# One core's transformer network: the last weight sum of a chunk's last pair on VectorE, and the activations' block sums queued behind the norm's factor

## The chip, the core and the metric

The kernel runs on one core of a Trainium2 chip. The core has a matrix engine (PE, TensorE), a vector engine (DVE, VectorE), an activation engine (ACT, ScalarE), a general engine (POOL, GpSimd) and a sync engine (SP) that here only issues DMAs. Each engine works through its own queue in order; between engines an instruction waits on semaphores. The metric is the device time of one execution in microseconds (us); less is better.

## The reference, cut to what matters

Input is a sequence of 512 tokens of width 1024. A first block (sparse attention beside an mLSTM, cross attention, one SwiGLU network) is followed by a second block of two layers, each with a half-step SwiGLU network ahead of its mixer and one behind it. The change is in three of these four networks: numbers 1, 2 and 4 in the order in which they run (`BLOCKED`). Each computes

```
h = h + 0.5 * swiglu(rms_norm(h, gain))
def swiglu(x, w_gate, w_up, w_down):      # x 512 x 1024, F = 2816
    return (silu(x @ w_gate) * (x @ w_up)) @ w_down
```

The rms norm is split: the gain goes into the activations, and the factor per token is multiplied in behind the products. Everything is float32.

## The kernel before, in words

**Exact products.** A float32 operand is split into a high and a low part (`split`, L125 to L136): ACT makes the high part (`whi` of a weight, `xh` or `sh` of activations; L129, L135), DVE the low part (`wlo`, `xl`, `sl`; L133, L136). A product is three matmuls (`mm3`, L175). So every weight tile of 128x1024 costs one ACT and one DVE instruction before PE can use it.

**The blocked networks** (`ffn_blocks`, L385 to L584). The hidden width is 22 row tiles. The first four (p = 0 to 3) are projected plainly, each as a gate product `pg` and an up product `pu` over the 512 tokens (24 matmuls of 512 columns each), and finished by `plain` (L507): DVE multiplies the gate by the factor `rb` (L510), ACT applies Silu (L511), DVE multiplies by the up part (L512), and the result is split into `hh` and `hl`. The other tiles are computed in pairs (`pair`, L465) by a 2x2 block scheme with seven products in place of eight: tokens are halved (LO, HI), and the width too. Seven products of 24 matmuls with 256 columns go to PE for a pair m, with sums of weights on one side and sums of activation blocks (`s1` to `s4`) on the other: s1 with the weight sum `wt`; a11 with b11; s4 with b22; then, behind the last product of the pair before, s2 with `wt` after a second sum; a12 with b21 (PSUM tile B, `sc`); s3 with b12; and last a22 with `wt` after a third sum.

**The weight sum.** `wt` is one SBUF tile that changes twice. `sum_ahead` (L501) makes the first value on DVE. `add` (L436) then adds a block in place by DMAs with accumulation, issued by POOL, two of 256 KB each: `add(wt, m, 3)` behind the split for s1, `add(wt, m, 2)` behind the split for s2 (L485). The block that the last one adds, b21, is also loaded by SP into a tile of its own for the product B (`load`, L429). After each change the tile is split again. A chunk is a run of pairs between two down projections: pairs 2 to 3, 4 to 7, 8 to 10; so there are nine chunk ends in the three networks, with m = 3, 7, 10. At a chunk's end no pair follows whose products would lie between s3 and a22.

**The block sums.** `block_sums` (L405) makes the raw sums r1 to r4 of the activation blocks on DVE (L410 to L414), in two halves `kp`, and splits them into `sh` and `sl`. It needs only the new activations, so the scheduler puts it wherever DVE is free, which is before the norm's factor is there.

**What sets the order.** PE's order is written out by hand around the pairs (`order_pe`, `free_pe`). DVE, ACT, POOL and SP get theirs from a list scheduler with a cost model; `tc.issue_after(instruction)` keeps what is issued inside it behind that instruction. The norm's factor comes from a chain (`inv_rms_chain`, L232): sums of squares by matmuls with `ones` (L259), a power on POOL (L265), transposes with `ident` (L272), and the copy `rb` to SBUF on DVE (L245).

Of the kernel before, what the change touches and what calls it, by code (L numbers as in the profile page):

```python
# [12 lines left out]
ALU = mybir.AluOpType  # L13
# [3 lines left out]
D = 1024  # L17
# [33 lines left out]
def kernel(ctx: ExitStack, tc: tile.TileContext, t: dict, out: bass.AP):  # L51
    nc = tc.nc
# [44 lines left out]
    xa, x = load_x()  # L97
# [19 lines left out]
    def v(name, j):  # L117
        o = VOFF[name] + j
        return vec[:, o : o + 1]
# [115 lines left out]
    def inv_rms_chain(state, first, second):  # L235

        if not state:
            for j in range(KT):
                square_acc(x[j], j, state, eng=nc.vector)
        got = []  # L240

        def finish():
            rt, pb = rms_rows(got[0], WHOLE)
            rb = act_p.tile([P, S], F32, tag="rb", bufs=2, name=nm("rb"))
            nc.vector.tensor_copy(rb, pb)  # L245
            got[:] = [rt, rb]

        chain.append([first, lambda: got.append(rms_sums(state, 1e-6, WHOLE))])
        chain.append([second, finish])
        return got  # L250
# [131 lines left out]
    LO, HI = HALVES  # L382
    CHUNKS = ((0, 4), (4, 8), (8, FT // 2))

    def ffn_blocks(fp, xs, st, gname, wg, wu, wd, out_cb, head=2, tail=0, step=None):  # L385
# [12 lines left out]
        sums = {}  # L398
# [5 lines left out]

        def block_sums(kp):  # L405
            r1, r2, r3, r4 = (raw[q, kp] for q in (1, 2, 3, 4))
            for kk in range(2):
                k, c = 2 * kp + kk, slice(256 * kk, 256 * kk + 256)
                g1, g2 = v(gname, k), v(gname, 4 + k)
                nc.vector.tensor_scalar(r1[:, c], x[4 + k][:, HI], g2, None, ALU.mult)  # L410
                nc.vector.scalar_tensor_tensor(r1[:, c], x[k][:, HI], g1, r1[:, c], ALU.mult, ALU.subtract)
                nc.vector.scalar_tensor_tensor(r2[:, c], x[k][:, LO], g1, r1[:, c], ALU.mult, ALU.subtract)
                nc.vector.scalar_tensor_tensor(r4[:, c], x[4 + k][:, LO], g2, r2[:, c], ALU.mult, ALU.subtract)
                nc.vector.tensor_tensor(r3[:, c], x[k][:, LO], x[k][:, HI], ALU.subtract)  # L414
            split(r1, *sums[1, kp])
            split(r2, *sums[2, kp], -1.0)
            split(r4, *sums[4, kp])
            for kk in range(2):
                c = slice(256 * kk, 256 * kk + 256)
                split(r3[:, c], *(t_[:, c] for t_ in sums[3, kp]), v(gname, 2 * kp + kk))  # L420

# [42 lines left out]

        def pair(m, p):  # L465

# [17 lines left out]
            product(A, s2, load_w(None, D, wt), False)  # L484
            add(wt, m, 2)  # L485
            nc.vector.tensor_tensor(of_half(c2, 0), of_half(c2, 0), lanes(A), ALU.subtract)
            B = ps_tile("sc")
            product(B, a12, load_w(None, D, load(m, 2)), True)
            nc.vector.tensor_tensor(of_half(c1, 0), of_half(c1, 0), lanes(B), ALU.add)
# [52 lines left out]
        for p in range(4):  # L542
            if p < len(pss):
                pg, pu = pss[p]
            else:
                pg = mm_tile()
                proj(pg, load_w(wg[p], D), xs)
                pu = at_tile()
                proj(pu, load_w(wu[p], D), xs)
            plain(p, pg, pu)  # L550
            if p in (2, 3):
                block_sums(p - 2)
        for ci, (m0, m1) in enumerate(CHUNKS):
            last = ci == len(CHUNKS) - 1
            ms = range(max(m0, 2), m1)
            for p in range(len(hs) if ci == 0 else 0, 2 * (m1 - m0)):
                if ci == 0:
                    hs.append(h_tiles(p))
                else:
                    hs[p:p + 1] = [h_tiles(p)]  # L560
            gens = {m: pair(m, 2 * (m - m0)) for m in ms}
            order_pe()
# [109 lines left out]
    free_pe()  # L672
    rt, rb = got
    for ps, nme in zip(first, ("kc", "vc")):
# [883 lines left out]
    free_pe()  # L1558
    rt, rb = got
    Wl, PTs = None, []  # L1560
# [179 lines left out]
```

## Time and profile before

| what | us |
|---|---|
| median of 3 runs | 2802.57 |
| lowest and highest run | 2800.8, 2808.41 |
| the profiled execution's own time | 2799.68 |
| its span in the trace | 2797.9 |
| PE busy | 2707.0 |
| DVE busy | 1732.4 |
| ACT busy | 1214.6 |
| POOL busy | 439.5 |

The span is what the trace covers of the profiled execution; some 2 us lie around it. The mean granted clock of TensorE is 0.986 of full speed. Busy times overlap across engines, and only what PE waits for shows directly in the time.

### The profile page before, as it was taken

The numbers are of one execution on the slowest core, as the hardware profiler recorded it, in microseconds if no ns is written. First come the engines' busy times: TensorE is split into PE (matmuls) and PEld (weight loads), VectorE is DVE, ScalarE is ACT, GpSimd is POOL, SyncE is SP. The second block draws the span as 40 slices with busy tenths as digits, with TensorE's granted clock in tenths as the row PEclk, the third lists the DMA queues.
The fourth block names the chain that finished last, engine by engine and source line by source line (L and its number), as shares of the span: only waits on it lengthen the run. The fifth ranks groups of instructions, "written<-read, shape, count | busy, mean of one in ns | idle before, by whom it ended". The sixth has DMA issues, their size and how long they took to land.

```text
span 2797.9 us, 40467 instructions
## 1 busy us (share of the span) xinstructions
PE 2707.0 (97%) x15856; PEld 2332.1 (83%) x15856; DVE 1732.4 (62%) x2608; ACT 1214.6 (43%) x1967; POOL 439.5 (16%) x559
## 2 busy tenths in 40 slices
PE   9999999999998999999899999999999998999998
PEld 6877988888887898986688989898888874899997
DVE  7666564642437666669885666744444489666665
ACT  6676544422334434442344434443222366443434
POOL 0133132100002110122220101200000136211112
PEclk9999999999998999999999999999999999999999
DMA  6313321323322454536333545323232320254552
GB/s 201 98 47 99 120 68 53 98 80 111 97 84 97 121 129 117 135 112 163 96 117 106 144 121 123 111 89 100 83 113 89 100 69 8 81 132 116 140 131 73
DMA packets 118051, 291.84 MB, mean 104 GB/s; under 512 B 13111, under 2 KB 20279, under 8 KB 117860
## 3 DMA queue, kind: packets, MB, share of 16 engines
q1 hardware_dynamic: 100700, 258.43, 29.1%
q0 software_dynamic: 15552, 28.32, 6.6%
q10 hardware_dynamic: 1608, 2.52, 0.3%
q8 instruction: 124, 2.03, 0.3%
q14 instruction: 67, 0.55, 0.1%
HBM read 284.91 MB, written 4.30 MB: 103 GB/s over the span
## 4 chain that ended last, share of the span: by engine, by line
PE 67%; DVE 9%; DMA 4%; issue 4%; ACT 2%; POOL 0%; SPq 0%; DVEq 0%; ACTq 0%; POOLq 0%
PE mm L175 23%; PE sc L175 19%; PE tr L175 17%; PE po L175 6%; DMA wb<-wu 3%; DVE wlo L133 2%; ACT whi L129 1%; DVE c L1340 1%; DVE rm L1507 1%; DVE xl L136 1%; DVE conv L1340 1%; PE po L1537 1%; DMA R<-glscr 0%; DMA glscr<-gl 0%; PE sc L160 0%
## 5 line engine op out<-in xcount | busy, mean ns | idle before, releaser
L129 ACT ACTIVATE whi<-wraw 128x1024 fp32r<-128x1024 f32 (+3 forms) x386 | 370.4, 970 | 756.4 <-PE sc L175 248.5
L133 DVE TENSOR_TENSOR wlo<-wraw,whi 128x1024 fp32r<-128x1024 f32 (+4 forms) x451 | 450.9, 1015 | 283.3 <-ACT whi L129 282.7
L175 PE MATMUL mm<-xh,whi 128*128 128x256 f32 (+1 forms) x1016 | 334.7, 330 | 5.9 <-ACT whi L129 5.9
L129 ACT ACTIVATE whi<-wb 128x1024 fp32r<-128x1024 f32 x189 | 199.9, 1058 | 321.7 <-PE mm L175 86.5
L175 PE MATMUL mm<-xl,whi 128*128 128x256 f32 (+1 forms) x1016 | 333.8, 329 | 5.5 <-DVE xl L136 5.5
L175 PE MATMUL mm<-xh,wlo 128*128 128x256 f32 (+1 forms) x1016 | 333.7, 328 | 0.0
L133 DVE TENSOR_TENSOR wlo<-wb,whi 128x1024 fp32r<-128x1024 f32 x189 | 230.8, 1221 | 111.3 <-ACT whi L129 107.2
L175 PEld LDWEIGHTS mm<-xh,whi 128*128 128x128 f32 x1016 | 194.7, 192 | 23.3 <-ACT whi L129 6.5
L175 PEld LDWEIGHTS mm<-xl,whi 128*128 128x128 f32 x1016 | 194.8, 192 | 22.3 <-DVE xl L136 6.8
L175 PEld LDWEIGHTS mm<-xh,wlo 128*128 128x128 f32 x1016 | 194.8, 192 | 15.9 <-DVE wlo L133 0.5
L175 PE MATMUL sc<-xh,whi 128*128 128x512 f32 (+1 forms) x576 | 200.8, 349 | 0.0
L175 PE MATMUL sc<-xh,wlo 128*128 128x512 f32 (+1 forms) x576 | 199.8, 347 | 0.0
L175 PE MATMUL sc<-xl,whi 128*128 128x512 f32 (+1 forms) x576 | 199.8, 347 | 0.0
L438 POOL DMA_DIRECT2D wb<-wg x54 | 47.2, 874 | 745.2 <-DVE wlo L133 739.5
L218 POOL TENSOR_TENSOR sqacc<-sq,sq 128x512 f32<-128x512 f32 (+1 forms) x11 | 16.7, 1516 | 862.0 <-issue 671.6
L175 PE MATMUL mm<-sh,whi 128*128 128x256 f32 (+1 forms) x448 | 132.6, 296 | 19.9 <-ACT c L453 18.9
L175 PE MATMUL tr<-xl,whi 128*128 128x512 f32 (+1 forms) x416 | 147.7, 356 | 3.9 <-DVE xl L136 3.9
L175 PE MATMUL tr<-xh,whi 128*128 128x512 f32 (+1 forms) x416 | 148.5, 357 | 1.0 <-ACT xh L135 1.0
L175 PE MATMUL tr<-xh,wlo 128*128 128x512 f32 (+1 forms) x416 | 147.8, 355 | 0.0
L175 PE MATMUL mm<-sl,whi 128*128 128x256 f32 (+1 forms) x448 | 132.7, 296 | 0.0
L175 PE MATMUL sc<-hh,whi 128*128 128x512 f32 (+1 forms) x347 | 132.5, 382 | 0.0
L175 PE MATMUL mm<-sh,wlo 128*128 128x256 f32 (+1 forms) x448 | 132.1, 295 | 0.0
(573 smaller groups left out, 7114.2 us busy)
## 6 DMA issues: line engine op xcount, KB each, us to landing
wraw<-wg SPq DMA_DIRECT2D x56, 512.0 KB, 3.5
wraw<-wu SPq DMA_DIRECT2D x56, 512.0 KB, 3.5
wb<-wg SPq DMA_DIRECT2D x108, 256.0 KB, 4.2
wb<-wu SPq DMA_DIRECT2D x108, 256.0 KB, 5.0
wraw<-wd SPq DMA_DIRECT2D x56, 384.0 KB, 3.0
wraw<-wd SPq DMA_DIRECT2D x56, 320.0 KB, 2.9
wb<-wg POOLq DMA_DIRECT2D x54, 256.0 KB, 4.1
wb<-wu POOLq DMA_DIRECT2D x54, 256.0 KB, 7.4
```

What stands on the lines that cost most here:

```text
L129: last_hi[0] = nc.scalar.activation(hi[:, sl], src[:, sl], AF.Copy)
L133: nc.vector.tensor_tensor(lo[:, sl], src[:, sl], f32(hi[:, sl]), ALU.subtract)
L136: nc.vector.scalar_tensor_tensor(lo, src, scale, f32(hi), ALU.mult, ALU.subtract)
L175: nc.tensor.matmul(ps, a, b, start=start and c == 0, stop=stop and c == 2, skip_group_check=more)
L218: eng.tensor_tensor(state["acc"][:, ts], state["first"][:, ts], sq[:, ts], ALU.add)
L438: nc.gpsimd.dma_start(w[:, 512 * lane : 512 * lane + 512], src, accum_op=ALU.add)
L1340: nc.vector.scalar_tensor_tensor(d, tap(k), v("w_dw", 31 * j + k), d, ALU.mult, ALU.add)
L1507: nc.vector.tensor_tensor_scan(rm[:, :L][:, ::-1], ob[:, 1 : L + 1][:, ::-1], ob[:, 1 : L + 1][:, ::-1], 1.0, ALU.mult, ALU.bypass)
L1537: nc.tensor.matmul(po[64 * hx : 64 * hx + 64, j * P :], vsh[:, j, c0 : c0 + 64], PTs[hx][:, o : o + n_], start=j == 0, stop=j == NT - 1)
```

## The change

The copy `rb` is handed out of the norm's chain as an instruction. `block_sums` takes a list of steps (half, part), and it is called with all DVE and ACT instructions kept behind that copy: r1 of both halves at p = 2; at p = 3 r2 and r4 of both halves (r4 is split first), then r3. In `pair`, a flag marks a chunk's last pair; there the third value of `wt` is made by a DVE addition of the loaded b21, and the two accumulating DMAs are not issued.

```diff
@@ -242,8 +242,7 @@
         def finish():
             rt, pb = rms_rows(got[0], WHOLE)
             rb = act_p.tile([P, S], F32, tag="rb", bufs=2, name=nm("rb"))
-            nc.vector.tensor_copy(rb, pb)
-            got[:] = [rt, rb]
+            got[:] = [rt, rb, nc.vector.tensor_copy(rb, pb).ins]
 
         chain.append([first, lambda: got.append(rms_sums(state, 1e-6, WHOLE))])
         chain.append([second, finish])
@@ -402,22 +401,26 @@
         def h_tiles(p):
             return [fp.tile([P, S], F32R, tag=f"h{q}{p}", name=nm(f"h{q}{p}")) for q in "hl"]
 
-        def block_sums(kp):
-            r1, r2, r3, r4 = (raw[q, kp] for q in (1, 2, 3, 4))
-            for kk in range(2):
-                k, c = 2 * kp + kk, slice(256 * kk, 256 * kk + 256)
-                g1, g2 = v(gname, k), v(gname, 4 + k)
-                nc.vector.tensor_scalar(r1[:, c], x[4 + k][:, HI], g2, None, ALU.mult)
-                nc.vector.scalar_tensor_tensor(r1[:, c], x[k][:, HI], g1, r1[:, c], ALU.mult, ALU.subtract)
-                nc.vector.scalar_tensor_tensor(r2[:, c], x[k][:, LO], g1, r1[:, c], ALU.mult, ALU.subtract)
-                nc.vector.scalar_tensor_tensor(r4[:, c], x[4 + k][:, LO], g2, r2[:, c], ALU.mult, ALU.subtract)
-                nc.vector.tensor_tensor(r3[:, c], x[k][:, LO], x[k][:, HI], ALU.subtract)
-            split(r1, *sums[1, kp])
-            split(r2, *sums[2, kp], -1.0)
-            split(r4, *sums[4, kp])
-            for kk in range(2):
-                c = slice(256 * kk, 256 * kk + 256)
-                split(r3[:, c], *(t_[:, c] for t_ in sums[3, kp]), v(gname, 2 * kp + kk))
+        def block_sums(steps):
+            for kp, part in steps:
+                r1, r2, r3, r4 = (raw[q, kp] for q in (1, 2, 3, 4))
+                for kk in range(2):
+                    k, c = 2 * kp + kk, slice(256 * kk, 256 * kk + 256)
+                    g1, g2 = v(gname, k), v(gname, 4 + k)
+                    if part == 1:
+                        nc.vector.tensor_scalar(r1[:, c], x[4 + k][:, HI], g2, None, ALU.mult)
+                        nc.vector.scalar_tensor_tensor(r1[:, c], x[k][:, HI], g1, r1[:, c], ALU.mult, ALU.subtract)
+                    elif part == 2:
+                        nc.vector.scalar_tensor_tensor(r2[:, c], x[k][:, LO], g1, r1[:, c], ALU.mult, ALU.subtract)
+                        nc.vector.scalar_tensor_tensor(r4[:, c], x[4 + k][:, LO], g2, r2[:, c], ALU.mult, ALU.subtract)
+                    else:
+                        nc.vector.tensor_tensor(r3[:, c], x[k][:, LO], x[k][:, HI], ALU.subtract)
+                        split(r3[:, c], *(t_[:, c] for t_ in sums[3, kp]), g1)
+                if part == 1:
+                    split(r1, *sums[1, kp])
+                elif part == 2:
+                    split(r4, *sums[4, kp])
+                    split(r2, *sums[2, kp], -1.0)
 
         def of_sum(q):
             return [tuple(t_[:, 256 * (k % 2) : 256 * (k % 2) + 256] for t_ in sums[q, k // 2]) for k in range(4)]
@@ -462,7 +465,8 @@
 
         first_sum = {}
 
-        def pair(m, p):
+        def pair(m, p, ends):
+
 
             if m not in first_sum:
                 first_sum[m] = sum_ahead(m)
@@ -482,10 +486,14 @@
             nc.scalar.activation(of_half(c2, 0), lanes(E), AF.Copy)
             yield
             product(A, s2, load_w(None, D, wt), False)
-            add(wt, m, 2)
+            if not ends:
+                add(wt, m, 2)
             nc.vector.tensor_tensor(of_half(c2, 0), of_half(c2, 0), lanes(A), ALU.subtract)
             B = ps_tile("sc")
-            product(B, a12, load_w(None, D, load(m, 2)), True)
+            b21 = load(m, 2)
+            product(B, a12, load_w(None, D, b21), True)
+            if ends:
+                nc.vector.tensor_tensor(wt, wt, b21, ALU.add)
             nc.vector.tensor_tensor(of_half(c1, 0), of_half(c1, 0), lanes(B), ALU.add)
             if m + 1 < FT // 2:
                 first_sum[m + 1] = sum_ahead(m + 1)
@@ -548,8 +556,9 @@
                 pu = at_tile()
                 proj(pu, load_w(wu[p], D), xs)
             plain(p, pg, pu)
-            if p in (2, 3):
-                block_sums(p - 2)
+            if p >= 2:
+                with tc.issue_after(got[2]):
+                    block_sums([(0, 1), (1, 1)] if p == 2 else [(0, 2), (1, 2), (0, 3), (1, 3)])
         for ci, (m0, m1) in enumerate(CHUNKS):
             last = ci == len(CHUNKS) - 1
             ms = range(max(m0, 2), m1)
```

Two further lines take `got[:2]` where `got` was unpacked.

At a chunk's end on DVE, first network, pair 3, before: `wlo_1659` is the low part of `wt` (`wb_1640`) for s2, `wlo_1663` that of b21, `wlo_1668` that of b12 for s3, `wlo_1670` that of the final `wt`; L486 takes s2's product out of PSUM.

```order
L133 TENSOR_TENSOR wlo_1659_9039<-wb_1640_8865,whi_1658_9038 128x1024
L454 TENSOR_TENSOR c_1624_8705<-c_1624_8705 128x512
L133 TENSOR_TENSOR wlo_1663_9074<-wb_1661_9070,whi_1662_9073 128x1024
L133 TENSOR_TENSOR hl5_1615_8689<-c_1624_8705,hh5_1614_8688 128x512
L133 TENSOR_TENSOR wlo_1668_9111<-wb_1642_8869,whi_1667_9110 128x1024
L133 TENSOR_TENSOR wlo_1670_9145<-wb_1640_8865,whi_1669_9144 128x1024
L452 TENSOR_TENSOR c_1623_8704<-c_1623_8704,rb_1567_8507 128x512
L486 TENSOR_TENSOR c_1646_8908<-c_1646_8908,mm_1650_8941 128x2x256
```

The same place with the change:

```order
L133 TENSOR_TENSOR wlo_1659_9039<-wb_1640_8865,whi_1658_9038 128x1024
L457 TENSOR_TENSOR c_1624_8705<-c_1624_8705 128x512
L496 TENSOR_TENSOR wb_1640_8865<-wb_1640_8865,wb_1661_9068 128x1024
L133 TENSOR_TENSOR wlo_1663_9072<-wb_1661_9068,whi_1662_9071 128x1024
L133 TENSOR_TENSOR hl5_1615_8689<-c_1624_8705,hh5_1614_8688 128x512
L133 TENSOR_TENSOR wlo_1668_9110<-wb_1642_8869,whi_1667_9109 128x1024
L133 TENSOR_TENSOR wlo_1670_9144<-wb_1640_8865,whi_1669_9143 128x1024
L455 TENSOR_TENSOR c_1623_8704<-c_1623_8704,rb_1567_8507 128x512
L491 TENSOR_TENSOR c_1646_8908<-c_1646_8908,mm_1650_8941 128x2x256
```

The addition (L496) stands three instructions ahead of where the final `wt` is split, and L486 is now L491; the rest keeps its order.

At the head of network 4 on DVE, from the copy `rb` on, before (L510 and L512 are `plain`'s multiplications of p = 0, 1, 2):

```order
L245 COPY rb_3699_22189<-po_3698_22184 128x512
L510 TENSOR_TENSOR c_3724_22234<-mm_3683_21933,rb_3699_22189 128x512
L510 TENSOR_TENSOR c_3727_22242<-mm_3685_21935,rb_3699_22189 128x512
L512 TENSOR_TENSOR c_3724_22234<-tr_3684_21934,c_3724_22234 128x512
L512 TENSOR_TENSOR c_3727_22242<-tr_3686_21936,c_3727_22242 128x512
L133 TENSOR_TENSOR hl0_3726_22239<-c_3724_22234,hh0_3725_22238 128x512
L133 TENSOR_TENSOR hl1_3729_22247<-c_3727_22242,hh1_3728_22246 128x512
L510 TENSOR_TENSOR c_3730_22250<-sc_3687_22131,rb_3699_22189 128x512
L133 TENSOR_TENSOR wlo_3762_22422<-wb_3753_22379,whi_3761_22421 128x1024
L512 TENSOR_TENSOR c_3730_22250<-sc_3688_22132,c_3730_22250 128x512
```

With the change the copy is followed by r1's first halves and r3 (eight instructions L411 and L417) and the two L518 that were L510 of p = 0 and 1; then:

```order
L412 SCALAR_TENSOR_TENSOR sraw_3700_22204<-x_789_3625,vec_73,sraw_3700_22204 128x256 x2
L412 SCALAR_TENSOR_TENSOR sraw_3712_22216<-x_789_3625,vec_73,sraw_3712_22216 128x256 x2
L136 SCALAR_TENSOR_TENSOR sl30_3708_22212<-sraw_3706_22210,vec_73,sh30_3707_22211 128x256 x2
L136 SCALAR_TENSOR_TENSOR sl31_3720_22224<-sraw_3718_22222,vec_73,sh31_3719_22223 128x256 x2
L414 SCALAR_TENSOR_TENSOR sraw_3703_22207<-x_789_3625,vec_73,sraw_3700_22204 128x256
L133 TENSOR_TENSOR wlo_3762_22416<-wb_3753_22373,whi_3761_22415 128x1024
L414 SCALAR_TENSOR_TENSOR sraw_3703_22207<-x_789_3625,vec_73,sraw_3700_22204 128x256
L520 TENSOR_TENSOR c_3724_22228<-tr_3684_21928,c_3724_22228 128x512
L414 SCALAR_TENSOR_TENSOR sraw_3715_22219<-x_789_3625,vec_73,sraw_3712_22216 128x256
L520 TENSOR_TENSOR c_3727_22236<-tr_3686_21930,c_3727_22236 128x512
L414 SCALAR_TENSOR_TENSOR sraw_3715_22219<-x_789_3625,vec_73,sraw_3712_22216 128x256
L133 TENSOR_TENSOR sl10_3702_22206<-sraw_3700_22204,sh10_3701_22205 128x512
```

All 30 DVE instructions of a network's block sums stand behind `rb` now, with `plain`'s multiplications and the weights' low parts between them; the first low part for s1 (`sl10`) is the twenty-sixth instruction behind the copy, and the last multiplication of p = 3 (L520) stands behind all of them.

On ACT, at the place where pair 2 of network 4 hands on its first PSUM tiles: `hh3` is the high part of p = 3, L478 copies the product a11 with b11 (`mm_3760`) out of the PSUM tile that s2 then continues, and L475 and L482 copy E (`tr_3757`). Before:

```order
L511 ACTIVATE c_3741_22340<-c_3741_22340 128x512
L129 ACTIVATE whi_3766_22483<-wb_3752_22378 128x1024
L129 ACTIVATE hh3_3742_22344<-c_3741_22340 128x512
L129 ACTIVATE whi_3770_22518<-wb_3769_22515 128x1024
L475 ACTIVATE c_3756_22387<-tr_3757_22388 128x2x256
L129 ACTIVATE whi_3775_22555<-wb_3754_22382 128x1024
L478 ACTIVATE c_3755_22386<-mm_3760_22420 128x2x256
L129 ACTIVATE whi_3780_22592<-wb_3772_22547 128x1024
```

With the change (L482 is what L478 was, L486 what L482 was):

```order
L519 ACTIVATE c_3730_22244<-c_3730_22244 128x512
L519 ACTIVATE c_3741_22326<-c_3741_22326 128x512
L129 ACTIVATE hh2_3731_22248<-c_3730_22244 128x512
L129 ACTIVATE whi_3780_22586<-wb_3772_22541 128x1024
L486 ACTIVATE c_3756_22381<-tr_3757_22382 128x2x256
L129 ACTIVATE hh3_3742_22330<-c_3741_22326 128x512
L482 ACTIVATE c_3755_22380<-mm_3760_22414 128x2x256
```

`hh3` stood four places ahead of the copy that frees s2's PSUM tile, and now stands right ahead of it; both Silu (L519) and `hh2` have come into this stretch. On PE, networks 1 and 2 now run s1, a11 and the first seven matmuls of s4 ahead of p = 3's up product, which stood behind the first three matmuls of s1; the rest of PE's order stays.

## Rows read from the trace of the kernel before

**Rows 1.** The page, part 1: busy us of each engine, share, instructions.

```profile
PE 2707.0 (97%) x15856; PEld 2332.1 (83%) x15856; DVE 1732.4 (62%) x2608; ACT 1214.6 (43%) x1967; POOL 439.5 (16%) x559
```

**Rows 2.** Waits of PE, whole span: line and releaser: us, times, longest.

```profile
PE mm L175 <- ACT c L453: 18.9, 6, 4.7
PE sc L259 <- DVE sqacc L220: 7.5, 1, 7.5
```

**Rows 3.** Timeline of PE at two chunk ends: start, duration, instruction [idle before].

```profile
962.56 0.36 PE L175 MATMUL mm<-sh,whi 128*128 128x256 f32 x1 [2.33 <-ACT c L453]
...
1642.28 0.55 PE L175 MATMUL mm<-sh,whi 128*128 128x256 f32 x1 [4.68 <-ACT c L453]
...
1647.33 0.42 PE L175 MATMUL mm<-sh,wlo 128*128 128x256 f32 x1
```

**Rows 4.** Windows of PE: stretch, length, busy (count), granted clock, DMA share, GB/s.

```profile
900.00:915.00 15.00, 12.24 (x50) 0.75 0.29 74
...
1085.00:1100.00 15.00, 11.59 (x64) 0.89 0.51 166
1506.00:1520.00 14.00, 11.31 (x67) 0.88 0.35 110
1640.00:1660.00 20.00, 17.72 (x89) 0.83 0.28 86
...
2635.00:2655.00 20.00, 17.30 (x92) 0.91 0.32 98
```

**Rows 5.** Timeline of DVE at the first chunk end.

```profile
948.58 1.22 DVE L133 TENSOR_TENSOR wlo<-wb,whi 128x1024 fp32r<-128x1024 f32 x1
...
959.99 1.23 DVE L133 TENSOR_TENSOR wlo<-wb,whi 128x1024 fp32r<-128x1024 f32 x1 [6.10 <-ACT whi L129]
...
961.73 0.68 DVE L486 TENSOR_TENSOR c<-c,mm 128x512 f32<-128x512 f32 x1
```

**Rows 6.** Timeline of ACT there: b21's high part, then the final sum's.

```profile
949.24 1.04 ACT L129 ACTIVATE whi<-wb 128x1024 fp32r<-128x1024 f32 x1
...
958.89 1.06 ACT L129 ACTIVATE whi<-wb 128x1024 fp32r<-128x1024 f32 x1 [5.78 <-DMA wb<-wu]
```

**Rows 7.** Timeline of POOL there: the two accumulating DMAs' issues.

```profile
950.10 0.87 POOL L438 DMA_DIRECT2D wb<-wg  x1 [11.43 <-DVE wlo L133]
950.64 1.22 POOL L438 DMA_DIRECT2D wb<-wu  x1
```

**Rows 8.** Timeline of PE at the heads of networks 1, 2 and 4.

```profile
902.76 1.84 PE L259 MATMUL sc<-ones,sqacc 128*128 128x1 f32 x8 [7.50 <-DVE sqacc L220]
...
920.05 0.28 PE L175 MATMUL tr<-sh,whi 128*128 128x256 f32 x1
...
934.14 0.28 PE L175 MATMUL mm<-sh,whi 128*128 128x256 f32 x1
...
1482.96 0.28 PE L175 MATMUL mm<-sh,whi 128*128 128x256 f32 x1
...
2478.48 0.28 PE L175 MATMUL tr<-sh,whi 128*128 128x256 f32 x1
...
2481.36 0.28 PE L175 MATMUL mm<-sh,whi 128*128 128x256 f32 x1
```

**Rows 9.** Timeline of DVE: block sums of network 1, and two copies `rb`.

```profile
894.33 0.68 DVE L133 TENSOR_TENSOR sl<-sraw,sh 128x512 fp32r<-128x512 f32 x1
894.93 0.47 DVE L413 SCALAR_TENSOR_TENSOR sraw<-x,vec,sraw 128x256 f32<-128x256 f32 x1
895.33 0.68 DVE L136 SCALAR_TENSOR_TENSOR sl<-sraw,sh 128x512 fp32r<-128x512 f32 x1
...
910.94 0.68 DVE L245 COPY rb<-sc 128x512 f32<-128x512 f32 x1
...
2460.20 0.69 DVE L245 COPY rb<-po 128x512 f32<-128x512 f32 x1 [1.92 <-PE po L272]
```

**Rows 10.** Groups by line, DVE, 881 to 903.5 us: count | busy us, mean ns.

```profile
L410 DVE TENSOR_SCALAR sraw<-x,vec 128x256 f32<-128x256 f32 x4 | 1.4, 340 | 0.0
```

More of the change, by code (lines that the diff above doesn't have):

```diff
@@ L560, in ffn_blocks @@
                     hs[p:p + 1] = [h_tiles(p)]
-            gens = {m: pair(m, 2 * (m - m0)) for m in ms}
+            gens = {m: pair(m, 2 * (m - m0), m == ms[-1]) for m in ms}
             order_pe()
@@ L672 @@
     free_pe()
-    rt, rb = got
+    rt, rb = got[:2]
     for ps, nme in zip(first, ("kc", "vc")):
@@ L1558 @@
     free_pe()
-    rt, rb = got
+    rt, rb = got[:2]
     Wl, PTs = None, []
```

## The prediction

> **What bounds the kernel now.** I read the page first. PE is busy for 2707.0 us of the span [rows 1], so an edit on another engine can gain only what PE waits for, and can lose whatever new wait it makes. Next I read the list of PE's waits [rows 2]. Two entries touch lines of this change: a product's matmuls waiting six times, 18.9 us in all, by a release put down to an ACT copy (L453), and one wait of 7.5 us for the sums of squares.
>
> The timeline of PE shows where the six are: two of them, 2.33 and 4.68 us, are the first matmul of s3 in a chunk's last pair [rows 3]. All six are of that form, in the first and second chunk of each network; the third chunk's end has none. The name L453 misleads, since that copy is done before anyone can need it. The queues around the first end tell the true cause. DVE splits `wt` for s2 at 948.58 [rows 5], POOL issues the two accumulating DMAs at 950.10 and 950.64 [rows 7], and ACT sits idle for 5.78 us with the final sum's high part at the head of its queue, until 958.89, released by the DMA [rows 6]. DVE, behind it, starts the low part at 959.99 after 6.10 us of idleness, and only then, at 961.73, takes s2's product out of PSUM (L486) [rows 5]. s3 overwrites that PSUM tile, so PE starts at 962.56. The final sum itself is needed later: it holds up the wrong instruction by standing ahead of it in two queues.
>
> A wait also costs clock. The windows show full speed lost around the ends: granted clock 0.89, 0.88, 0.83 and 0.91 [rows 4]. After 4.68 us of waiting the 24 matmuls of s3 take from 1642.28 to 1647.33 plus a last one of some 0.2 [rows 3], 5.26 us, where an undisturbed product of that form takes 2.88 (from 2478.48 to 2481.36) [rows 8]. One minus the clock, times the length of the window, is 1.65 + 1.68 + 3.40 + 1.80 = 8.5 us for the four windows; part of it lies in the waits themselves. Counted by the matmuls behind the waits I take 7.
>
> **Part A, the addition on DVE.** Eighteen accumulating DMAs and their issues go, nine additions of 128x1024 come. I price one by the low part of a weight, the same form with two inputs: 1.22 us [rows 5], of which the next instruction overlaps 0.08, so 1.14. b21 is no new wait: ACT makes its high part at 949.24 already [rows 6], so it has landed when the addition runs at about 950.4. Queued behind the addition stand the low parts of b21 and b12, the final `wt`, and L486. The final sum is ready at 951.6. Counting back from 960, where B ends and PE comes to s3, by 2.88 a product, s2 ran from 954.3 to 957.2. The final sum's high part then waits only for a buffer that frees when a22 of the pair before ends, at 954.3; with 1.04 for it, 1.22 for the low part and 0.6 for the multiplication ahead of L486, DVE comes to L486 at 957.3, as s2's product is just there, and PSUM is free at about 958. So the wait goes whole at this end, with about 2 us to spare, and the 1.14 us of DVE are covered by that slack; without it they would cost 1.14 at each of six ends. Since the others have the same queues, all six go. b21's load buffer comes free about 1.2 us later, which delays a weight load of the down projection; I cost that at nothing for the same slack, and at most at 1.2 us each. So part A brings 18.9 us if the clock gives nothing back, 27 with the windows' 8.5, 26 with 7; I take 26, since a clock that fell behind a wait has no such cause left.
>
> The two DMAs of one sum end some 8.2 us after the second issue (950.64 to 958.89) [rows 6, 7]; that is the duration used. The Trainium skill, DMA: Bandwidth & Descriptors, section on the anatomy of one DMA by the gpsimd path, gives 2.0 us plus bytes over 436e3, for 256 KB an estimate of 2.6 us. By that the sum would be there at 953.3, before its buffer, part A would be worth nothing, and the total would be the heads' loss alone. The trace does not agree, and the measurement decides.
>
> **Part B, the block sums behind `rb`.** What it removes: in network 1 these sums ran ahead of the squares on DVE, and PE waited 7.50 us at 902.76 for the squares [rows 8], in a window at a clock of 0.75 [rows 4], so 3.75 us of full speed, most of it in the wait; about 1.5 lies behind it. Up to 9 us go there, less what the last squares wait for on their own account.
>
> What it adds: 30 DVE instructions between the copy `rb` and the pairs. Prices as start to start: 0.60 for 512 columns (894.33 to 894.93), 0.40 for 256 (894.93 to 895.33) [rows 9], 0.26 for the one-input form (340 ns less 0.08) [rows 10], 1.14 for a weight. In order of the queue up to s1's second low part: copy 0.6, four L411 1.04, four L417 1.6, two L518 1.2, four L412 1.6, four low parts of r3 1.6, four L414 1.6, a weight 1.14, two L520 1.2, two low parts of r1 1.2: 12.8 us, and 12.2 to the first.
>
> In **network 1** the copy starts at 910.94 [rows 9], so s1 can start at 923.1; PE wanted it at 920.05 [rows 8], and now has no up product in between: 3.1 us of wait. Up to the first low part of r4 follow four L415 1.6, two weights 2.28 and five of 512 columns 3.0: 19.7 us, at 930.6. PE, done with s1 and a11 (2.88 each) from 923.1 on, is there at 928.9: 1.7 more. Behind the up product and the rest of s4, s2 waits about 0.3 for the copy out of its PSUM tile, which stands behind `hh3` on ACT. s2 comes about 5.1 us late against 934.14 [rows 8], up to 6.2 with some clock lost. Against the 7.5 to 9 removed I take minus 3, between minus 4 and 0, since I can't see when the last squares are ready.
>
> **Network 2** has the same queue, s2 at 1482.96 before [rows 8], and no wait to lose: 5.1 to 6.4 us, I take 6.
>
> In **network 4** the copy starts at 2460.20 [rows 9]. The whole queue to the last multiplication of p = 3 adds, to the 12.8, six weights 6.84, ten of 512 columns 6.0 and four L415 1.6: 27.2 us, at 2487.4. Here the up product is done early, so nothing fills the gaps: s4, wanted at 2478.48 [rows 8], waits about 2.5 for its first low part, 1.5 for its second. Then on ACT `hh2`, a weight's high part (1.04 [rows 6]), two PSUM copies and `hh3` at 0.5 to 0.6 each lie between that multiplication and s2: 2489.9 against 2481.36 [rows 8], 8.5 late, a last wait of 4.5. At the chunk ends waits of such a length took clock; with that, 7 to 11 us, I take 9.5.
>
> Sum: 26 gained, 3 gained, 6 and 9.5 lost, so 13.5 off 2799.68, the profiled execution's own time: 2786.2. The median of the runs lies 2.9 above that execution: **2789**. By the bounds (27 + 4 - 5 - 7 = 19, and 19 + 0 - 6.4 - 11 = 1.6) between 2783.5 and 2801 as medians.
>
> **The rivals.**
>
> *The heads eat the gain.* The ends return only their waits, network 1 gains nothing, and 2 and 4 cost their upper bounds: 1.6 off, 2801, within 0.3% (8.4 us, about what a measurement of this kernel can tell from no change). For it: every number of part B is a queue sum in which one late ACT step adds. Against: the waits at the ends are whole and the slack is 2 us. It decides once the ends give under 19 or the heads cost over 20.
>
> *The heads cost nothing.* DVE has more room than my sums say, or PE's later arrival is absorbed: then 26 + 9 = 35 off, 2768. For it: DVE stands idle for a third of the span [rows 1]. Against: behind `rb` the queue is one unbroken chain.
>
> *Slower: half clock through the heads.* Each head gets two or three waits of 1.5 to 4.5 us in a row, in place of one or none. One product of 24 matmuls costs 5.26 - 2.88 = 2.4 us more at the low clock of 1.2 GHz [rows 3, 8]. If from s1 to s3 seven products' worth per head ran at it, that is 17 us, 6 of them absorbed by the very waits: 11 times three is 33, and the time 2789 + 33 = 2822. It decides from 7.3 us a head on (22 in all), some three products beyond what the waits absorb. For it: 0.83 after 4.68 us [rows 4]. Against: the six waits together lost 7 us, each under 2.6. The Trainium skill, TensorE: Matmul & The Clock Gate, part 1, says the throttled state is the default and that activity lifts it. By that rule the heads' waits decide this rival; the trace agrees so far that the clock was 0.75 around the wait of 7.5 us [rows 4], and shows no head with several shorter ones.
>
> *The addition is late.* If b21 landed after the split for s2, the addition would wait in DVE's queue as the DMA did in ACT's: nothing from part A, 12.5 lost, 2815. For it: b21 is loaded for B alone, which comes later. Against: 949.24 [rows 6], 1.2 us ahead of the addition's turn; it decides from about 2 us of delay.
>
> **How the numbers follow.** Forecast 0.63 (2783 to 2794), the heads eat the gain 0.22, heads free 0.07, half clock 0.05, late addition 0.03. Faster by over 0.3% are the forecast and the free heads, 0.70; the same is the second case, 0.22; slower are the last two, 0.08. For 8 in 10 the range takes the forecast, nearly all of the second and some of the third: 2776 to 2804.
>
> **What would show it.** Right: no idle of ACT on a DMA ahead of the final `wt` at m = 3, 7, 10, no wait of s3, clock 1.00 there; no 7.5 us wait for squares; new waits of s1 near 3 us in networks 1 and 2 and of s2 over 4 in network 4. Wrong: s3 still waiting, on DVE or on a load; a head's s2 late by more than 11 us; the granted clock under 0.85 across a whole head; or waits for r1 to r4 that sum to under 5 us.

## The result

The changed kernel takes 2787.1 us (median of 4 runs, 2782.41 to 2788.24), the kernel before 2805.21 beside it (4 runs, 2800.8 to 2808.41): a ratio of 0.9933, 95% interval 0.9913 to 0.9954. The forecast was 2789, faster by over 0.3%. The profiled execution took 2788.24 us, 11.4 less than that of before.

PE's work is the same, and the page's first part says so for after (busy us, share, instructions), to be read beside [rows 1]. PE is busy for 1.7 us more in a span 11.5 us shorter, so what left the span on balance is waiting; slow clock went at the chunk ends and came at the heads.

```profile
PE 2708.7 (97%) x15856; PEld 2331.6 (84%) x15856; DVE 1740.2 (62%) x2617; ACT 1213.0 (44%) x1967; POOL 422.4 (15%) x541
```

The list of PE's waits, after (us in total, times, longest). The two rows of [rows 2] are gone, and four of the new ones belong to the heads:

```profile
PE tr L175 <- DVE sl L133: 7.1, 4, 2.4
PE mm L175 <- ACT c L482: 2.6, 1, 2.6
...
PE po L175 <- DVE c L518: 0.8, 1, 0.8
PE tr L175 <- DVE c L520: 0.6, 1, 0.6
```

The first chunk end, after: the timeline of DVE (start, duration, instruction [idle before]), with the addition (L496), the final sum's low part and the subtraction that frees PSUM (L491).

```profile
948.85 1.22 DVE L496 TENSOR_TENSOR wb<-wb,wb 128x1024 f32<-128x1024 f32 x1
...
955.44 1.23 DVE L133 TENSOR_TENSOR wlo<-wb,whi 128x1024 fp32r<-128x1024 f32 x1 [1.64 <-ACT whi L129]
956.58 0.68 DVE L455 TENSOR_TENSOR c<-c,rb 128x512 f32<-128x512 f32 x1
957.30 0.69 DVE L491 TENSOR_TENSOR c<-c,mm 128x512 f32<-128x512 f32 x1
```

The addition starts right behind the instruction ahead of it, so b21 was there. The 6.10 us of idleness in [rows 5] have become 1.64. ACT's high part ahead of it starts at 954.35, when s2 has just begun on PE (954.22); that fits the wait for a free buffer which the prediction reckoned, though the profile names no releaser there. L491 ends at 957.99. PE's timeline at that place shows s3 without a wait, 2.0 us later:

```profile
959.98 0.28 PE L175 MATMUL mm<-sh,whi 128*128 128x256 f32 x1
```

The windows of PE, after (stretch, length, busy, granted clock, DMA share, GB/s): one over the squares in network 1, two over chunk ends, and one over the head of network 4. They answer to [rows 4].

```profile
897.00:912.00 15.00, 14.99 (x74) 1.00 0.49 127
957.00:972.00 15.00, 15.00 (x103) 1.00 0.37 106
...
1629.00:1649.00 20.00, 20.00 (x123) 1.00 0.45 140
2465.00:2485.00 20.00, 14.29 (x79) 0.66 0.52 106
```

And PE's timeline at the three heads, after, to be read beside [rows 8]: the squares; s1 in network 1; s2 in network 1; s1's wait, the up product's wait and s2 in network 2; s4's two waits, s2 and the product behind it in network 4.

```profile
900.03 0.95 PE L258 MATMUL sc<-ones,sqacc 128*128 128x1 f32 x8
...
916.08 0.35 PE L175 MATMUL tr<-sh,whi 128*128 128x256 f32 x1 [0.57 <-DVE c L520]
917.97 0.38 PE L175 MATMUL tr<-sl,whi 128*128 128x256 f32 x1 [1.54 <-DVE sl L133]
...
933.96 0.38 PE L175 MATMUL mm<-sh,whi 128*128 128x256 f32 x1
...
1464.73 0.58 PE L175 MATMUL tr<-sl,whi 128*128 128x256 f32 x1 [2.38 <-DVE sl L133]
...
1473.93 0.50 PE L175 MATMUL po<-xh,whi 128*128 128x512 f32 x1 [0.76 <-DVE c L518]
...
1481.54 0.28 PE L175 MATMUL mm<-sh,whi 128*128 128x256 f32 x1
...
2467.78 0.38 PE L175 MATMUL tr<-sl,whi 128*128 128x256 f32 x1 [2.07 <-DVE sl L133]
2470.12 0.58 PE L175 MATMUL tr<-sl,whi 128*128 128x256 f32 x1 [1.07 <-DVE sl L133]
2476.68 0.58 PE L175 MATMUL mm<-sh,whi 128*128 128x256 f32 x1 [2.57 <-ACT c L482]
...
2481.96 0.28 PE L175 MATMUL sc<-xh,whi 128*128 128x256 f32 x1
```

**Where the time went, by stage.** PE runs the same products in the same order in both kernels but for the moved up product. So I took the start of one product in both traces, formed the difference (after minus before), and read how that difference changes across a stage. A head is taken from ahead of the factor's transposes (in network 1 from directly ahead of the squares) to the product B behind s2, so that the clock behind s2's wait is in it; the chunk ends from there to behind the network's second chunk. The same reading was made of every experiment below, always against the first profile of before.

| profile | up to network 1's squares | network 1's head | network 2's head | network 4's head | six chunk ends |
|---|---|---|---|---|---|
| after | +4.9 | -5.0 | +5.6 | +10.8 | -27.3 |
| e1, addition alone | +1.1 | 0.0 | 0.0 | 0.0 | -26.7 |
| e2, block sums alone | +3.4 | -5.0 | +5.6 | +9.7 | -2.4 |
| e11, the same again | -1.5 | -5.0 | +5.7 | +10.8 | -7.9 |
| e3, addition and network 1 | +3.6 | -5.0 | 0.0 | 0.0 | -27.3 |
| e4, DMA kept, split late | +5.2 | +1.4 | 0.0 | 0.0 | -25.8 |
| e5, after with r3 late | -0.2 | -5.6 | +4.4 | +5.8 | -27.4 |
| e6, e3 with r3 late | -0.4 | -5.6 | 0.0 | 0.0 | -27.3 |
| e7, addition and network 4 | -1.2 | 0.0 | 0.0 | +9.7 | -27.3 |
| e8, five additions | +1.7 | 0.0 | 0.0 | 0.0 | -16.8 |
| e9, order of use only | -0.4 | 0.0 | 0.0 | 0.0 | -27.3 |
| e10, before again | +3.2 | 0.0 | 0.0 | 0.0 | -2.3 |

What lies ahead of the squares holds nothing of the change, and it differs by up to 6.7 us between executions, by 4.9 between two profiles of one kernel (e2 and e11). So a single execution's total says less than its stages. For after they sum to -5.0 + 5.6 + 10.8 - 27.3 = -15.9. The last column takes in short waits between the ends; the 0.6 us by which e1 differs from after are such waits, and at the six ends themselves the two kernels gain the same.

### The profile page after: what moved, and what is told of

It is laid out like the page before. It is cut to its first block, busy times and chain, and to the rows that moved or that the text cites. A ratio compares the mean times of both kernels' runs of the same rounds, so it can differ in the third digit from the quotient of the medians.

```text
span 2786.4 us, 40428 instructions
## 1 busy us (share of the span) xinstructions
PE 2708.7 (97%) x15856; PEld 2331.6 (84%) x15856; DVE 1740.2 (62%) x2617; ACT 1213.0 (44%) x1967; POOL 422.4 (15%) x541
## 4 chain that ended last, share of the span: by engine, by line
PE 74%; DVE 7%; issue 2%; ACT 1%; DMA 1%; POOL 0%; SPq 0%; DVEq 0%; ACTq 0%
PE mm L175 27%; PE sc L175 20%; PE tr L175 19%; PE po L175 6%; DVE wlo L133 1%; DVE c L1349 1%; DVE rm L1516 1%; PE po L1546 1%; DVE conv L1349 1%; ACT whi L129 0%; DMA R<-glscr 0%; PE sc L1337 0%; DMA glscr<-gl 0%; DVE xl L136 0%; PE sc L160 0%
## 5 line engine op out<-in xcount | busy, mean ns | idle before, releaser
L441 POOL DMA_DIRECT2D wb<-wg x45 | 39.5, 878 | 718.5 <-DVE wlo L133 714.6
L175 PE MATMUL tr<-sl,whi 128*128 128x256 f32 (+1 forms) x448 | 131.6, 294 | 7.1 <-DVE sl L133 7.1
L175 PE MATMUL sc<-hl,whi 128*128 128x512 f32 (+1 forms) x347 | 131.6, 379 | 0.0
```

The source lines that it names most:

```text
L175: nc.tensor.matmul(ps, a, b, start=start and c == 0, stop=stop and c == 2, skip_group_check=more)
L441: nc.gpsimd.dma_start(w[:, 512 * lane : 512 * lane + 512], src, accum_op=ALU.add)
```

## The experiments

**e1, the addition alone.** Part A without part B.

```diff
-            add(wt, m, 2)
+            if not ends:
+                add(wt, m, 2)
...
-            product(B, a12, load_w(None, D, load(m, 2)), True)
+            b21 = load(m, 2)
+            product(B, a12, load_w(None, D, b21), True)
+            if ends:
+                nc.vector.tensor_tensor(wt, wt, b21, ALU.add)
```

> The addition on VectorE at the nine chunk ends alone; the block sums stay as before. My theory: the six waits of s3 (18.9 us) and the slow clock behind them (some 7 us) go, 26 to 27 us less than before, ratio 0.9905; the wait of 7.5 us for the squares in network 1 stays, networks 2 and 4 show no new waits at their heads. That is some 10 us faster than the changed kernel. Rival: the gain at the ends needs the heads' new order as well (pairs that start later find their loads landed); then under 19 us less, and s3 still waits at some of the ends.

Measured: 2773.32 us (2771.73 to 2774.56, 4 runs), ratio 0.9898 (0.9885 to 0.9911). The ends give 26.7, the wait for the squares stays, as the list of PE's waits shows, and no head has a new one:

```profile
PE sc L259 <- DVE sqacc L220: 7.0, 1, 7.0
```

Part A needs nothing from part B, and alone it beats the changed kernel by 13.8 us between the medians. The rival falls.

**e2 and e11, the block sums alone**, twice. The flag for a chunk's last pair is always false.

```diff
-            gens = {m: pair(m, 2 * (m - m0), m == ms[-1]) for m in ms}
+            gens = {m: pair(m, 2 * (m - m0), False) for m in ms}
```

> The block sums behind the norm's factor alone; all pairs keep the accumulating DMAs. My theory: network 1's head gains about 5 us, network 2's loses 5.5, network 4's loses 10.8 with its slow clock: 11 us more than before, ratio 1.004, and the six waits of s3 stand as they were, 18.9 us. Rival: the later block sums cost what they cost in the changed kernel only because the additions load VectorE too; then within 3 us of before.

> The block sums alone once more, one profile. By my theory the heads' waits repeat: network 1 gains 4 to 5 us, network 2 loses 5.5 to 6, network 4 loses 8.4 and 1 to 2.5 of clock, as in the first profile; what differs between the two profiles lies at other places (the first 870 us, the chunk ends). Rival: the heads' losses come and go with the execution; then network 4's s2 is under 6 us late.

Measured: 2805.18 us (2798.55 to 2814.03, 12 runs) beside 2802.95 of before (17 runs), ratio 1.0011 (1.0000 to 1.0023), so a loss of 0 to 6 us and not the 11 expected; the second profile's one execution took 2804.36. Yet the heads do what they do in the changed kernel, each within 1.1 us of it in both profiles: their rows sum to +10.3 and +11.5. What differs is the ends. In e2's list of PE's waits the six waits are there with 16.5 us, in e11's five with 14.1:

```profile
PE mm L175 <- ACT c L456: 16.5, 6, 4.4
```

```profile
PE mm L175 <- ACT c L456: 14.1, 5, 4.4
```

So the heads' losses are real and repeat (the rivals fall), while the total of this kernel is blurred by how much the ends lose in an execution.

**e10, the kernel before once more.** No edit.

> The kernel before once more, one profile. The median of the block sums alone lay 2 us above before while its profile adds up to 10 at the heads. If executions of one kernel differ by where the clock falls behind the six waits of s3, this profile shows the same six waits within 0.5 us each but another sum of slow stretches than 7 us behind them. If the waits themselves vary, they differ by over 0.5 us.

Measured: one execution, 2803.47 us. The list of waits has 16.5 us in place of 18.9 for the same six, and the timeline of PE shows that the fourth, 4.68 us in [rows 3], is 3.34 here:

```profile
PE mm L175 <- ACT c L453: 16.5, 6, 3.7
```

```profile
1647.31 0.36 PE L175 MATMUL mm<-sh,whi 128*128 128x256 f32 x1 [3.34 <-ACT c L453]
```

So waits themselves vary: two of the six differ by more than the 0.5 us that I gave as the line, the first (0.6 us) and this one. The DMA is a part of that: at that end its issue-to-release time is 7.72 us here, from the timelines of POOL and ACT,

```profile
1635.93 1.23 POOL L438 DMA_DIRECT2D wb<-wu  x1
```

```profile
1643.65 1.06 ACT L129 ACTIVATE whi<-wb 128x1024 fp32r<-128x1024 f32 x1 [5.65 <-DMA wb<-wu]
```

where the first profile of before has 8.18 at the same end, from POOL's issue and ACT's start there:

```profile
1630.44 1.23 POOL L438 DMA_DIRECT2D wb<-wu  x1
```

```profile
1638.62 1.06 ACT L129 ACTIVATE whi<-wb 128x1024 fp32r<-128x1024 f32 x1 [6.11 <-DMA wb<-wu]
```

**e4, the DMA kept, the split late.** No addition on DVE. The final sum's split is only queued behind the subtraction (`freed`) on DVE and behind the last Silu of the pair before (`before`) on ACT.

```diff
-            nc.vector.tensor_tensor(of_half(c2, 0), of_half(c2, 0), lanes(A), ALU.subtract)
+            freed = nc.vector.tensor_tensor(of_half(c2, 0), of_half(c2, 0), lanes(A), ALU.subtract).ins
...
-            product(A, a22, load_w(None, D, wt), False)
+            with ExitStack() as behind:
+                behind.enter_context(tc.issue_after(freed))
+                if m - 1 in before:
+                    behind.enter_context(tc.issue_after(before[m - 1]))
+                w22 = load_w(None, D, wt)
+            product(A, a22, w22, False)
```

> The accumulating DMAs are all kept and VectorE adds nothing; only the split of the final weight sum is queued later, behind the subtraction that frees s3's PSUM tile on VectorE and behind the Silu of the pair before on ScalarE. Block sums as before. My theory, that the landing itself is early enough and only the queue order made s3 wait: the six waits go, 20 to 26 us less than before, ratio 0.991 to 0.993. Rival: the sum is needed when the DMA brings it, or the DMA's traffic holds the rest up: then a22 waits in place of s3, under 8 us less.

Measured: 2777.43 us (2777.33 to 2781.89, 4 runs), ratio 0.9917 (0.9904 to 0.9930); the ends give 25.8. The DMAs land as late as ever: at the first end POOL issues the second one at 957.16, and ACT's high part starts at 964.65 (timelines of POOL and ACT),

```profile
957.16 1.23 POOL L438 DMA_DIRECT2D wb<-wu  x1
```

```profile
964.65 1.06 ACT L129 ACTIVATE whi<-wb 128x1024 fp32r<-128x1024 f32 x1 [1.52 <-DMA wb<-wu]
```

7.5 us, but s3 no longer stands behind it, and no s3 waits; PE loses only 0.2 us at each of two ends, to a weight's low part that comes later. So the six waits came from the order in two queues and not from the sum being late. This is the strongest reading of the study: with the DMA untouched, reordering alone brings nearly all of part A. Of the 4 us between the medians of e4 and e1 the ends explain 0.9; another 1.4 stand in e4's profile at network 1's head, which the edit doesn't touch, and the rest stays open.

**e8, five additions.** e1 with the addition made five times over (b21 added and taken away), 4 x 1.14 = 4.56 us more of DVE's queue at each end.

```diff
-                nc.vector.tensor_tensor(wt, wt, b21, ALU.add)
+                for op in (ALU.add, ALU.subtract, ALU.add, ALU.subtract, ALU.add):
+                    nc.vector.tensor_tensor(wt, wt, b21, op)
```

> The addition alone, but as five VectorE instructions in place of one (b21 added, taken away and so on), 4.56 us more of VectorE's queue at each of the nine ends; block sums as before. My theory, by the slack of 2 us that I reckoned at a first chunk's end: s3 waits 2 to 2.6 us at six ends, 12 to 16 us more than with one addition plus some slow clock, about 2787 to 2793. Rival: the additions run while VectorE would wait for the pair before, so that the slack is larger: then no s3 waits and the time is within 3 us of the one addition, 2773 to 2776.

Measured: 2785.42 us (2784.36 to 2788.12, 4 runs), 12.1 above e1; the ends give 16.8 in place of 26.7. The time is near what I expected, just under it, the place is not. The timeline of DVE at the first end shows why: the scheduler let the subtraction (L487) pass the last addition (L493),

```profile
958.98 1.22 DVE L493 TENSOR_TENSOR wb<-wb,wb 128x1024 f32<-128x1024 f32 x1
960.12 0.68 DVE L487 TENSOR_TENSOR c<-c,mm 128x512 f32<-128x512 f32 x1
960.72 0.68 DVE L454 TENSOR_TENSOR c<-c 128x512 f32<-128x512 f32 x1
961.32 1.22 DVE L493 TENSOR_TENSOR wb<-wb,wb 128x1024 f32<-128x1024 f32 x1
```

so s3 waits only 0.3 to 0.6 us at three ends, and the work comes late one step further on, at the first down projection, in the list of waits (six of these seven; e1 has the other, 0.5 us):

```profile
PE sc L175 <- DVE wlo L133: 4.8, 7, 0.7
```

The slack is thus not measured alone. What holds is that one addition is covered and five are not.

**e3, the addition, and the block sums behind the factor in network 1 alone.** In the other two, `block_sums_free` is the function of before.

```diff
-            if p >= 2:
+            if p >= 2 and gname == "ffn1_norm_0":
                 with tc.issue_after(got[2]):
                     block_sums([(0, 1), (1, 1)] if p == 2 else [(0, 2), (1, 2), (0, 3), (1, 3)])
+            elif p >= 2:
+                block_sums_free(p - 2)
```

> The addition at all chunk ends, and the block sums behind the norm's factor in network 1 alone (networks 2 and 4 as before). My theory: 26.5 us from the ends and 5 us from network 1's head, 31 to 32 us less than before, ratio 0.989, faster than either kernel; no wait for the squares in network 1, none of s1, s4, s2 in networks 2 and 4. Rival: what network 1 gains is given back later, at its first chunk end, since its pairs start with late loads; then no faster than the addition alone (26 us).

Measured: 2770.03 us (2768.28 to 2775.84, 4 runs), ratio 0.9890 (0.9875 to 0.9904). By the stages network 1 gives 5.0, as said, and the first ends give what they give elsewhere, so nothing is handed back. Against e1 the medians differ by 3.3 us, in runs that overlap.

**e7, the addition, and network 4 alone.** As e3, with `gname == "ffn2_norm_1"`.

> The addition at the chunk ends, and the block sums behind the factor in network 4 alone; networks 1 and 2 as before. My theory: 10.8 us more than the addition alone, of which 8.4 is s2 coming late and 2.4 the clock behind it: about 2784; the wait of 7.5 us for the squares in network 1 is there. Rival: the three heads' losses are not additive (the median of the block sums alone was only 2 us above before, not 10): then within 4 us of the addition alone, 2773 to 2777.

Measured: 2781.96 us (2780.72 to 2786.87, 4 runs), 8.6 above e1, ratio to before 0.9933 (0.9918 to 0.9948). The stage has 9.7, the list of waits both of its marks:

```profile
PE sc L258 <- DVE sqacc L220: 7.5, 1, 7.5
...
PE mm L175 <- ACT c L499: 2.6, 1, 2.6
```

The heads add up as far as they were tried: network 1 gains 5.0 us alone (e3) and with the others, network 4 loses 9.7 alone and 9.7 to 10.8 with the others, with the addition and without it. Network 2 was not moved alone.

**e9, the order of use alone.** The addition, and the sums in the changed order but not behind the factor.

```diff
-                with tc.issue_after(got[2]):
-                    block_sums([(0, 1), (1, 1)] if p == 2 else [(0, 2), (1, 2), (0, 3), (1, 3)])
+                block_sums([(0, 1), (1, 1)] if p == 2 else [(0, 2), (1, 2), (0, 3), (1, 3)])
```

> The addition at the chunk ends and the block sums in the changed order of use, but not kept behind the norm's factor. My theory, that the place behind the factor makes both the gain in network 1 and the losses in networks 2 and 4, and the order among the sums next to nothing: as the addition alone, 2771 to 2776, with the wait of 6 to 7.5 us for the squares in network 1 and no wait of s1, s4 or s2. Rival: the order of use matters by itself; then the squares' wait shrinks or new waits of s1 come without the factor, and the time is over 4 us away from 2773.

Measured: 2775.72 us (2773.36 to 2776.9, 4 runs), ratio 0.9899 (0.9882 to 0.9915). No head differs from before, and PE's timeline has the wait for the squares:

```profile
902.35 0.56 PE L258 MATMUL sc<-ones,sqacc 128*128 128x1 f32 x2 [7.25 <-DVE sqacc L220]
```

So the place behind the factor makes both gain and losses of part B, and the order among the sums alone changes nothing.

**e5, r3 queued late.** The changed kernel with r3's sums and splits behind p = 3's last low part (`done`).

```diff
             if p >= 2:
                 with tc.issue_after(got[2]):
-                    block_sums([(0, 1), (1, 1)] if p == 2 else [(0, 2), (1, 2), (0, 3), (1, 3)])
+                    block_sums([(0, 1), (1, 1)] if p == 2 else [(0, 2), (1, 2)])
+                if p == 3:
+                    with tc.issue_after(done):
+                        block_sums([(0, 3), (1, 3)])
```

> The changed kernel with one thing moved: r3's two halves and their splits (16 VectorE instructions of 256 columns with the order's doubles, 3.2 us of queue) are queued behind the last low part of p = 3; s3 needs them last. My theory, that VectorE's queue behind the norm's factor times the heads: networks 1 and 2 come to s1 without the wait of 1 to 2.4 us and lose 3.2 us less each, network 4's last multiplication of p = 3 comes 4.3 us earlier, so its s2 is about 4 late in place of 8.4, and the slow clock behind it shrinks: 10 to 13 us less than the changed kernel, about 2775. Rival: ScalarE's queue or the PSUM tiles time the heads, not VectorE's sums: under 4 us less, about 2784, and s2 of network 4 still 8 us late.

Measured: 2775.11 us (2772.48 to 2777.35, 4 runs), ratio 0.9905 (0.9890 to 0.9920), 12 below the changed kernel between medians of different sets of runs. The heads give 6.8 of it (0.6, 1.2 and 5.0); the rest no stage of the change shows. (What moved is eight instructions in each network, not 16; at 0.40 they are the 3.2 us that I gave.) Network 4's s2 comes 4.2 us late in place of 8.4, as DVE's queue said. In networks 1 and 2 the waits of s1 are gone, but PE's timeline shows s2 waiting for the copy out of its PSUM tile instead, in all three networks:

```profile
926.82 0.39 PE L176 MATMUL mm<-sh,whi 128*128 128x256 f32 x1 [2.06 <-ACT c L483]
...
1473.42 0.39 PE L176 MATMUL mm<-sh,whi 128*128 128x256 f32 x1 [2.06 <-ACT c L483]
...
2466.99 0.41 PE L176 MATMUL mm<-sh,whi 128*128 128x256 f32 x1 [3.53 <-ACT c L483]
```

and 1.6 us of slow clock behind each. My theory holds for network 4. For networks 1 and 2 the rival is right in part: with DVE out of the way, ACT's queue (`hh3` ahead of the copy) is the next to end late, and of the 3.2 us that I expected in each it leaves 0.6 and 1.2.

**e6, the addition, network 1 alone, r3 late.** e3 and e5 together.

> The addition at the chunk ends, and the block sums behind the factor in network 1 alone, r3 queued late there. My theory: 26.5 from the ends, 5 from network 1 as measured with the addition, and 3.2 more from r3: about 34 to 36 us less than before and 3 less than the kernel that has the two without r3's move, some 2767. Rival: network 1's remaining loss has another cause; then no different from that kernel, 2770.

Measured: 2767.41 us (2764.85 to 2769.86, 4 runs), ratio 0.9878 (0.9863 to 0.9893): the fastest of the study, about 20 us under the changed kernel and 35 under before. By the stages it gains 27.3 at the ends and 5.6 in network 1. Only 0.6 of that is more than e3 has at its head, so the 3 us that I expected from r3 there are not shown; that the total came out as expected, with medians 2.6 apart, is luck.

## Why the prediction was right, and where its sizes were off

**Chunk ends.** Said: the waits go whole, with clock 26 us, between 19 and 27. Measured: 27.3 against the first profile of before, 25.0 against the second (e10), no s3 waits, clock 1.00. Of the 27.3, 18.9 are the waits and 8.4 the clock, so the windows' 8.5 was the better count and the 7 was short. The cause named, a release put down to the wrong ACT instruction and a subtraction held up behind the final sum in two queues, is shown by e4. The slack of 2 us was reckoned from L491 ready at about 958 and s3 at 960; measured 957.99 and 959.98. The Trainium skill (DMA: Bandwidth & Descriptors, the anatomy of one DMA by the gpsimd path) has a fit that gives an estimate of 2.6 us for these 256 KB; the runs show 7.5 to 8.2, and the gain that this estimate would have denied was there.

**Network 1's head.** This step was mis-sized: 3 us gained, between 0 and 4, where four profiles of the changed head give 5.0 each. The new cost was about right (5.1 said; s2 comes 4.8 later against the squares). What was too small is the part removed: from before the squares to behind the next product the difference goes from +4.9 to -5.0, 9.9 us, where I took 7.5 to 9 less an unknown rest. The squares' matmuls take 0.95 us in place of 1.84 [rows 8], in windows with a granted clock of 1.00 in place of 0.75, and the last squares had no wait of their own.

Inside the new cost, s1 waits 2.1 us (3.1 said). s4's wait (1.7 said) differs between executions. In after it is not there: the head's window has a granted clock of 0.97 (0.73 over s1, 916.0 to 922.3), and PE comes to s4's second matmul, the first to need the low part, without idle time.

```profile
900.00:950.00 50.00, 47.83 (x302) 0.97 0.46 116
```

```profile
925.44 0.38 PE L175 MATMUL tr<-sl,whi 128*128 128x256 f32 x1
```

In e3, with the same head, the clock is 1.00 in that window, and s4 waits 1.46 us for its low part:

```profile
900.00:950.00 50.00, 46.35 (x304) 1.00 0.45 111
```

```profile
924.15 0.39 PE L175 MATMUL tr<-sl,whi 128*128 128x256 f32 x1 [1.46 <-DVE sl L133]
```

Both come to s2 4.8 us late. So DVE's queue set the time, as the sum had it, and what PE lost to the clock ahead of s4 cost nothing.

**Network 2's head.** Said 6 (5.1 to 6.4), measured 5.6. The wait of s1 is 2.38 and 0.76 stands at the up product, which the sum of 3.1 had in one piece. The 1.7 of s4 did not come as a wait here; s1's matmuls ran at a granted clock of 0.59 over 1464 to 1468 us instead.

**Network 4's head.** Said 9.5 (7 to 11), measured 10.8: s2 late by 8.4 (said 8.5), and 2.4 of clock. The split was wrong inside: I had s2 wait 4.5, and it waits 2.57. The rest of that gap went into s4, whose later matmuls ran at the low clock (0.66 over the window). s2's start was set by DVE and ACT, so the slow clock ahead of it cost nothing, and only the slow matmuls behind it did.

**The rivals.** The heads did eat 11 us net, not the 17 of the second case, and the ends gave their clock back. They are not free: e1 and e9 against after show that. Half clock through the heads did not come: 0.97 over 900 to 950 us and 1440 to 1500, and in network 4 it stops with s2's product. The addition was never late.

**The total.** The forecast moved by -13.5 us; the stages give -15.9 and the medians -18.1. The stages explain the sum but for 2.2 us, which lie within how executions differ. That 2789 came within 2 us of 2787.1 is in part luck: the gain was 4.6 us larger than forecast, and the median of before came out 2.6 us higher, with one run more, than the 2802.57 from which I started.

**Left open.** The block sums alone cost 0 to 6 us by the medians, where their heads lose 10.3 and 11.5. Their two profiles have 2.4 and 7.9 us less at the ends than the first profile of before, and the second profile of before has 2.3 less; whether later heads really shorten the DMA's waits or executions only differ, two profiles of each can't settle. Nor did I see why e5's median gains more than its heads.

## What to carry to other kernels

When an engine waits, look for what stands at the head of the queue that releases it, not only at the instruction named: here a transfer of 8 us did no harm once nothing urgent was queued behind it, and reordering alone was worth nearly as much as removing it. Work that hides under an earlier stage should be held back only where it is in someone's way: holding the block sums behind the factor gained 5 us in the one network where they delayed the squares, and lost 16 in the two where they delayed nothing. Before moving a block of short instructions behind a late event, add up the queue from that event to the first consumer on each engine; that sum was within 0.6 us of the measured lateness in all three networks.

## What the runs showed of the hardware that I had not expected

The same wait differs between executions of one kernel: 4.68 and 3.34 us at the same end, with 8.18 and 7.72 us from the DMA's issue to its release. A slow clock ahead of a wait that another engine sets is free: in network 4's head the window's granted clock was 0.66, and s2 came when DVE and ACT let it, 8.4 us late against 8.5 reckoned with full clock; in network 1 s2 came 4.8 us late at a clock of 0.97 (after) and at 1.00 (e3).
